# Where a sparse path's small steps stand on GpSimd, VectorE and SyncE in a two-layer encoder

## The chip, the cores and the metric

The kernel runs on one core of a Trainium2 chip. The metric is the device time of one execution in microseconds (us), the median of several runs; lower is better. The engines are TensorE (PE, with PEld for its weight loads), VectorE (DVE), ScalarE (ACT), GpSimd (POOL) and SyncE (SP, which here only issues DMAs).

## The reference

An encoder of two layers over 272 tokens (16 meta tokens and 256 of the input) of 1024 channels. Layer 0 mixes tokens with a gated recurrence, layer 1 with a convolution. Behind each mixer stands the same channel mixer, which picks 16 experts for each of 8 heads and each token, out of 16,384 experts; the change lies in it alone:

```python
def peer_block(xc, w_query, sub_keys, expert_u, expert_v):
    q = (xc @ w_query).reshape(c, PEER_HEADS, 2, PEER_HALF)
    scores = jnp.einsum('chpk,pnk->chpn', q, sub_keys.astype(q.dtype))
    s1, i1 = lax.top_k(scores[:, :, 0], PEER_TOPK)
    s2, i2 = lax.top_k(scores[:, :, 1], PEER_TOPK)
    cand = (s1[..., :, None] + s2[..., None, :]).reshape(c, PEER_HEADS, PEER_TOPK * PEER_TOPK)
    s, flat = lax.top_k(cand, PEER_TOPK)
    ...
    expert = idx1 * PEER_N_KEYS + idx2
    g = jax.nn.softmax(s.astype(jnp.float32), axis=-1).astype(xc.dtype)
    u = expert_u[expert]
    act = jax.nn.gelu(jnp.einsum('chkd,cd->chk', u, xc))
    v = expert_v[expert]
    return jnp.einsum('chk,chkd->cd', g * act, v)
```

The output is all tokens but the 16 meta tokens, in float32.

## The kernel before

**Dense and sparse.** Most tokens are computed densely: TensorE multiplies all 128 tiles of 128 experts of U with the tokens (240 of them), gates the result with one-hot matrices of the picks, and multiplies all 128 tiles of V. Some groups of 16 tokens take a sparse way instead, for the whole or for V alone: rows of U and V are fetched by expert number with indirect DMAs, which GpSimd issues. In layer 0 these groups are tokens 256 to 271 ("early"), 240 to 255 ("late") and 224 to 239 ("drawn"); in layer 1 they are 240 to 255 ("early"), 224 to 239 and 208 to 223 ("drawn"). Each group is a dictionary, `few` in the code. Those that lie below token 256 (all but the first) are called `near`.

**U1 and U2.** The 128 tiles of U are done by two calls of `linears`: tiles 0 to 63 (U1, with `u_store` as what is done to each result) and 64 to 127 (U2, with `u_out`). For each tile `load_split` loads a block of 128x1024 float32 (`raw`, four buffers, issued on SP's queue), ScalarE rounds it (`hi`, three buffers), and the rest `lo = raw - hi` (two buffers) is made by GpSimd for tiles 0 to 40 of U1 and by VectorE from tile 41 (`LO_FROM`) on. TensorE then does 16 matmuls on `hi` (L180, two sorts) and 8 on `lo`, in this order, for each tile. So a late `lo` stops TensorE between the `hi` and the `lo` matmuls of that tile.

**Beside U1**, VectorE picks the experts. `topk_steps` is a generator that yields after each step: 2H steps of maxima over scores, H steps over sums (`cand`), then one-hot steps that turn the found places into key numbers (casts `s`, `pu`, `pf`; comparisons `oh` on L929, products on L935, sums `idx` on L938). It runs whole for tokens 128 to 271 (`picked[0]`), then for tokens 256 to 271 by themselves with H = 1 (`few_topk`, layer 0 only), and for tokens 0 to 127 in the generator `slow`, whose last seven steps are taken one in a tile from tile 41 on. From the key numbers `few_ids` makes the row numbers of the gathers (`ids`).

**Small transfers.** The near groups have their key numbers spread over 128 partitions by way of DRAM: `few_spread` writes `pos` there and `few_fetch` reads it back, both on GpSimd's queue, at tiles 21 (`SPREAD`) and 24 of U1; `few_ids` follows. The softmax weights `z` go the same way near tile 60.

**Gathers.** For the early group, GpSimd fetches 16 rows of U (`few_rows`, L1028) and VectorE multiplies each with its token (`few_mult`, L1035): the first ten from tile 48 of U1 on (`few_dot`), the other six in U2 (`u_out`, L705 to L710), one in four tiles. In U2 `few_dump` also copies finished activations of the drawn groups to DRAM (L723, L724; one buffer `own`).

**The order** on each engine is set by a scheduler when the program is built: an instruction may be placed earlier than it is written, unless `tc.issue_after(x)` puts it behind instruction `x`. On the chip each engine takes its instructions strictly in that order, and waits on semaphores for its inputs.

Of the kernel before, what the change touches and what calls it, by code (L numbers as in the profile page):

```python
# [7 lines left out]
F32 = mybir.dt.float32  # L8
F32R = mybir.dt.float32r
F16 = mybir.dt.float16  # L10
U32 = mybir.dt.uint32
# [6 lines left out]
P = 128  # L18
# [44 lines left out]
class Trunk:  # L63
# [481 lines left out]
    def peer(self, layer, n, xs):  # L545
        tc, nc, a = self.tc, self.nc, self.a
# [9 lines left out]
        with tc.tile_pool(name=f"few{layer}", bufs=1) as kp:  # L556
# [5 lines left out]
            with tc.tile_pool(name=f"top{layer}", bufs=1) as sp:  # L562
# [31 lines left out]
                def u_store(j, ps):  # L594
                    if j == LO_FROM:
                        for few in early:
                            self.few_load(sp, few, "kept", 1)
                    if j >= LO_FROM and len(picked[-1]) == 2:
                        with tc.issue_after(self.dve_lo.ins):
                            try:  # L600
                                next(slow)
                            except StopIteration as end:
                                picked[-1] += end.value
                    k, step = divmod(3 * (j - DOTS_FROM), 4)
                    if early and 0 <= k < DOTS + AHEAD and step < 3:
                        with tc.issue_after(self.dve_lo.ins), tc.issue_after(self.lo_ins.ins):
                            self.few_dot(sp, early[0], k, DOTS, AHEAD)
                    last = nc.scalar.activation(act_a[:, j, :], ps, AF.Gelu_apprx_tanh)
                    i = j - (JA - 6 - 2 * len(picked))
                    t, odd = divmod(i, 2)  # L610
                    if 0 <= t < len(picked) and not odd:
                        c0, m, idx, fv = picked[t]
                        with tc.issue_after(last.ins), tc.issue_after(self.dve_lo.ins):
                            picked[t] = c0, m, idx, self.softmax(sp, fv, P)
                    if j == SPREAD:
                        with tc.issue_after(self.lo_ins.ins):
                            self.few_spread(near, "pos", picked[0][2])
                    if j == JA - 6 - len(picked):
                        with tc.issue_after(last.ins):
                            self.few_spread(near, "z", picked[0][3][:, None])  # L620
                    if j == SPREAD + 3:
                        with tc.issue_after(self.lo_ins.ins):
                            self.few_fetch(near, "pos")
                        for few in near:
                            self.few_ids(few, few["pos"])
                    if j == JA - 2:
                        with tc.issue_after(last.ins):
                            self.few_fetch(near, "z")
                    if t == len(picked) and not odd:
                        with tc.issue_after(last.ins):  # L630
                            for few in early:
                                if few not in near:
                                    self.few_soft(sp, few)
                    if 0 < t <= len(picked) and not odd:
                        with tc.issue_after(last.ins), tc.issue_after(self.mm.ins):
                            self.topk_out(*picked[t - 1], iT, ghT, glT)
                self.linears([U[j] for j in range(JA)], xs, nu, lambda j: FULL if j >= LO_FROM else (("p", 1024),), u_store)

            with tc.tile_pool(name=f"act1{layer}", bufs=1) as ap1:
# [55 lines left out]
                def u_out(i, ps):  # L695
# [7 lines left out]
                        nc.vector.tensor_tensor(w[:, :cd], w[:, :cd], tmp[:, :cd], op=OP.mult)  # L703
                    k, step = divmod(i - 2 + 4 * DOTS, 4)
                    if step == 0 and DOTS <= k < TOPK:  # L705
                        with tc.issue_after(self.dve_lo.ins):
                            early[0]["rows"][k] = self.few_rows(rp, early[0], a["u_rows"], 0, k, 1)
                    if step == 2 and DOTS <= k < TOPK:
                        with tc.issue_after(self.dve_lo.ins):
# [8 lines left out]
                    at[0] = upto  # L718

                def few_dump(few, j, j1):  # L720
                    own = rp.tile([P, 32, FEW], F32, tag="own", name="own", bufs=1)[:, :j1 - j]
                    act, o = (act_a, 0) if j < JA else (act_b, JA)
                    nc.gpsimd.tensor_copy(own, act[:, j - o:j1 - o, few["t0"]:few["t0"] + FEW])  # L723
                    nc.gpsimd.dma_start(few["table"][:, j:j1], own)  # L724
# [160 lines left out]
    def topk_steps(self, sp, sc, m, H, parts=1):  # L885
        nc = self.nc
        K = TOPK
        sv = sp.tile([P, H, 2, K], F32, tag="sv", name="sv", bufs=1)
        si = sp.tile([P, H, 2, K], U32, tag="si", name="si", bufs=1)
# [10 lines left out]
        cand = sp.tile([P, H, K, K], F32, tag="cand", name="cand", bufs=1)  # L900
# [3 lines left out]
        fi = sp.tile([P, H, K], U32, tag="fi", name="fi", bufs=1)  # L904
# [10 lines left out]
        s16 = sp.tile([P, 2, H, K], F16, tag="s16", name="s16", bufs=1)  # L915
        nc.vector.tensor_copy(s16[:m], si[:m].rearrange("p h a k -> p a h k"))
        pu = sp.tile([P, 2, H * K], U32, tag="pu", name="pu", bufs=1)
        fp = fi[:m].rearrange("p h k -> p (h k)")
        nc.vector.tensor_scalar(pu[:m, 0], fp, 4, None, op0=OP.logical_shift_right)
        nc.vector.tensor_scalar(pu[:m, 1], fp, 15, None, op0=OP.bitwise_and)  # L920
        pf = sp.tile([P, 2 * H * K, 2], F16, tag="pf", name="pf", bufs=1)
        nc.vector.tensor_copy(pf[:m], pu[:m].rearrange("p a n -> p (a n)")[:, :, None].to_broadcast([m, 2 * H * K, 2]))
        yield
        oh = sp.tile([P, 2 * H, K, K], F16, tag="cand", name="oh", bufs=1)
# [61 lines left out]
    def few_topk(self, sp, few, q):  # L986
# [18 lines left out]
    def few_spread(self, fews, key, src):  # L1005
        for few in fews:
            self.nc.gpsimd.dma_start(few[key, "far"].rearrange("h t a k -> t a h k"), src[few["t0"] - P:few["t0"] - P + FEW])

    def few_fetch(self, fews, key):
        for few in fews:  # L1010
            self.nc.gpsimd.dma_start(few[key], few[key, "far"].rearrange("h t a k -> (h t) a k"))

    def few_ids(self, few, pos):
        for i in range(2):
# [343 lines left out]
```

## Time and profile before

| | |
|---|---|
| device time, three runs | 1815.02, 1820.03, 1820.5 us; median 1820.03 |
| device time of the profiled execution | 1816.75 us |
| its span, first to last instruction | 1815.0 us, granted TensorE clock 0.987 |
| TensorE busy | 1744.5 us, 96% of the span |
| VectorE, ScalarE, GpSimd busy | 1506.4, 903.2, 545.1 us (83%, 50%, 30%) |

Rows of the profile have the start in us from the span's start, the duration in us, engine, line, operation, output and inputs, and how many instructions are merged; in square brackets stands how long the engine was idle ahead of it and what ended that. Rows of the list of waits have the total, the number of times and the longest. Line numbers are those of the kernel before.

### The profile page before, as it was taken

Reading aid. Unit: us, or ns where it says so; the run is one execution under the profiler, and the core shown is the slowest. Engines: PE = TensorE matmul, PEld = TensorE weight load, DVE = VectorE, ACT = ScalarE, POOL = GpSimd, SP = SyncE. Lnnn points to the kernel's source line nnn. Section 1 sums busy time; section 2 is a strip of 40 time slices with the busy share of each in tenths; the row PEclk is TensorE's granted clock in tenths of the full one; section 3 lists DMA queues with packets and bytes.
Section 4 is the critical chain, followed back from the end, with each engine's and each line's share of the span. In section 5 each row is a group of like instructions: output and inputs, shape, how many; then the busy total and the mean of one; then the engine's idle time right before and its main releaser. Section 6 shows DMA issues by size and latency. Waiting matters only on the chain.

```text
span 1815.0 us, 35001 instructions
## 1 busy us (share of the span) xinstructions
PE 1744.5 (96%) x13468; PEld 1686.4 (93%) x13468; DVE 1506.4 (83%) x2753; ACT 903.2 (50%) x1493; POOL 545.1 (30%) x374
## 2 busy tenths in 40 slices
PE   8999997999999999999998999599999999999997
PEld 7899997999999999999887899599999999999996
DVE  7786999899997888887799869918899978878776
ACT  6554443554445545875532645245554454545552
POOL 1102993210002545431000018681200015643310
PEclk9999998999999999999999999899999999999998
DMA  5445665866557989888441365368765569888884
GB/s 198 163 156 158 198 201 177 284 226 197 172 167 273 337 311 343 316 321 281 174 151 47 111 187 192 119 203 284 237 214 177 169 198 340 310 310 303 319 270 151
DMA packets 115720, 405.91 MB, mean 224 GB/s; under 512 B 14496, under 2 KB 15968, under 8 KB 115424
## 3 DMA queue, kind: packets, MB, share of 16 engines
q1 hardware_dynamic: 91632, 324.74, 53.6%
q0 software_dynamic: 23920, 78.93, 11.9%
q8 instruction: 106, 1.74, 0.4%
q14 instruction: 62, 0.51, 0.1%
HBM read 395.56 MB, written 8.05 MB: 222 GB/s over the span
## 4 chain that ended last, share of the span: by engine, by line
PE 78%; DVE 16%; issue 2%; ACT 1%; POOL 1%; DMA 1%; POOLq 0%; SPq 0%; DVEq 0%; ACTq 0%
PE u L180 36%; PE acc L742 21%; PE acc L746 13%; PE u L216 3%; DVE cy L1238 2%; DVE odd L1238 2%; DVE oh L935 1%; PE g L683 1%; PE g L684 1%; DVE lo L152 1%; POOL lo L152 1%; PE acc L781 1%; DVE x L363 1%; DVE si L898 1%; DVE r L896 0%
## 5 line engine op out<-in xcount | busy, mean ns | idle before, releaser
L145 ACT ACTIVATE hi<-raw 128x1024 fp32r<-128x1024 f32 x556 | 588.0, 1059 | 632.7 <-PE u L180 217.4
L152 DVE TENSOR_TENSOR lo<-raw,hi 128x1024 fp32r<-128x1024 f32 x474 | 577.9, 1224 | 175.0 <-PE u L180 77.2
L180 PE MATMUL u<-xs,hi 128*128 128x240 f32 (+2 forms) x4544 | 571.5, 278 | 0.6 <-DVE xs L379 0.6
L180 PEld LDWEIGHTS u<-xs,hi 128*128 128x128 f32 x4544 | 540.0, 190 | 1.5 <-DVE xs L379 1.2
L742 PE MATMUL acc<-w,hi 128*128 128x448 f32 (+1 forms) x1984 | 431.4, 359 | 2.4 <-DVE w L264 1.9
L742 PEld LDWEIGHTS acc<-w,hi 128*128 128x128 f32 x1984 | 354.4, 189 | 14.4 <-DVE w L264 2.3
L180 PE MATMUL u<-xs,lo 128*128 128x240 f32 (+2 forms) x2272 | 310.5, 278 | 34.5 <-POOL lo L152 21.7
L180 PEld LDWEIGHTS u<-xs,lo 128*128 128x128 f32 x2272 | 282.6, 190 | 36.8 <-POOL lo L152 22.5
L746 PEld LDWEIGHTS acc<-w,lo 128*128 128x128 f32 x2048 | 267.2, 191 | 8.7 <-DVE lo L152 4.9
L746 PE MATMUL acc<-w,lo 128*128 128x224 f32 (+1 forms) x2048 | 269.9, 273 | 3.0 <-DVE lo L152 2.8
L152 POOL TENSOR_TENSOR lo<-raw,hi 128x1024 fp32r<-128x1024 f32 x82 | 208.3, 2558 | 105.1 <-ACT hi L145 79.2
L1028 POOL DMA_INDIRECT rows<-peer_v,ids x96 | 151.1, 1574 | 222.0 <-DVE few_out L1069 138.7
L1028 POOL DMA_INDIRECT rows<-u_rows,ids x48 | 64.3, 1340 | 243.1 <-DVE rows L1035 201.1
L216 PE MATMUL u<-x,raw 128*128 128x272 f32 x480 | 114.5, 399 | 5.2 <-DMA x<-h 5.2
L216 PEld LDWEIGHTS u<-x,raw 128*128 128x128 f32 x480 | 92.9, 194 | 24.5 <-DMA raw<-w_in 5.1
L1069 DVE SCALAR_TENSOR_TENSOR few_out<-rows,act,few_out 128x1024 f32<-128x1024 f32 x90 | 115.2, 1280 | 0.0
L723 POOL COPY own<-act_b 128x512 f32<-128x512 f32 (+2 forms) x9 | 9.2, 1026 | 261.8 <-ACT act_b L699 250.1
L690 ACT ACTIVATE act_b<-g 128x488 f32<-128x488 f32 (+39 forms) x54 | 20.9, 388 | 108.1 <-DVE act_b L653 98.9
L1045 POOL DMA_INDIRECT act<-own,turn x48 | 59.5, 1239 | 25.3 <-DVE turn L1044 13.7
L666 DVE TENSOR_TENSOR AB<-iota,iT 128x2048 f16<-128x2048 f16 x54 | 65.8, 1221 | 0.1
L371 POOL TENSOR_SCALAR xs<-x,par 128x272 fp32r<-128x272 f32 (+1 forms) x4 | 3.5, 878 | 185.3 <-DVE x L363 185.3
L1035 DVE SCALAR_TENSOR_TENSOR rows<-rows,wide 128x1024 f32<-128x1024 f32 x48 | 58.6, 1221 | 0.0
(285 smaller groups left out, 1848.7 us busy)
## 6 DMA issues: line engine op xcount, KB each, us to landing
raw<-peer_u SPq DMA_DIRECT2D x256, 512.0 KB, 3.9
raw<-peer_v SPq DMA_DIRECT2D x248, 512.0 KB, 5.5
raw<-w_query SPq DMA_DIRECT2D x28, 512.0 KB, 3.6
raw<-pw SPq DMA_DIRECT2D x22, 512.0 KB, 3.5
raw<-w_in SPq DMA_DIRECT2D x16, 512.0 KB, 3.8
raw<-w_out SPq DMA_DIRECT2D x8, 512.0 KB, 4.2
raw<-peer_v SPq DMA_DIRECT2D x16, 256.0 KB, 4.3
wide<-wide SPq DMA_DIRECT2D x5, 512.0 KB, 5.0
```

Of the source, the lines that this page charges most:

```text
L145: self.act_hi = nc.scalar.activation(hi, raw, AF.Copy).ins
L152: i = e.tensor_tensor(lo[:, s], raw[:, s], hi[:, s].bitcast(F32), op=OP.subtract)
L180: self.mm = nc.tensor.matmul(ps[:, :n], l[:, k, :], xs(k, r)[:, :n], start=start, stop=stop)
L216: self.mm = self.nc.tensor.matmul(ps[:, :n], raw[:, k, :], x[:, k, :n], start=k == 0, stop=k == NB - 1)
L666: nc.vector.tensor_tensor(AB.rearrange("p x c (a b) -> p (x c) a b", b=2), keys, iT[:, c0 // HC].rearrange("p x c b -> p (x c) b")[:, :, N ...
L742: self.mm = nc.tensor.matmul(acc[b][:, :2 * n].rearrange("p (a t) -> p a t", a=2), hi, w[:, :, :n], start=j == 0, stop=j == NK - JG - 1, s ...
L746: self.mm = nc.tensor.matmul(main[b][:, :n], hi if p_ else lo, w[:, i, :n], start=False, stop=j == NK - 1 and not p_, skip_group_check=True)
L1028: self.nc.gpsimd.indirect_dma_start(out=t, out_offset=None, in_=table, in_offset=bass.IndirectOffsetOnAxis(ap=few["ids"][:, i, k:k + 1], a ...
L1035: self.nc.vector.scalar_tensor_tensor(t, t, 1.0, few["x"], op0=OP.mult, op1=OP.mult, accum_out=few["act"][:, k:k + 1])
L1045: self.nc.gpsimd.indirect_dma_start(out=few["act"][:, k:k + 1], out_offset=None, in_=few["table"].rearrange("p j (t o) -> (p j t) o", o=1) ...
L1069: nc.vector.scalar_tensor_tensor(few["out"], t, w, few["out"], op0=OP.mult, op1=OP.add)
L1238: nc.vector.scalar_tensor_tensor(z, h, w, z, op0=OP.mult, op1=OP.add)
```

## The change

1. In `u_out` the gather of rows 10 to 15 is ordered behind `lo_ins`, the last `lo` that GpSimd made (tile 40 of U1), instead of `dve_lo`, VectorE's latest.
2. The `pos` spreads and fetches are issued on SP's queue, behind the load of tile 21 and of tile 25, instead of on GpSimd's.
3. `few_topk` takes only three steps at once; the five that are left (the one-hot steps) follow from tile 41 on, two in a tile (`few_picked`), and `slow` waits until they are done. `few_ids` of the near groups stands behind VectorE's `lo` of tiles 42, 43 (and 44 in layer 1).
4. The scratch tiles of `topk_steps` have one set of buffers for H = 8 and one for H = 1, and the last piece of `few_dump` has buffers of its own.

```diff
+                    behind = [few for few in early if few.get("left")]
+                    if j >= LO_FROM and behind:
+                        with tc.issue_after(self.dve_lo.ins):
+                            for _ in range(min(2, behind[0]["left"])):
+                                self.few_picked(behind[0])
-                    if j >= LO_FROM and len(picked[-1]) == 2:
+                    elif j >= LO_FROM and len(picked[-1]) == 2:
...
                     if j == SPREAD:
-                        with tc.issue_after(self.lo_ins.ins):
-                            self.few_spread(near, "pos", picked[0][2])
+                        with tc.issue_after(self.last_load):
+                            self.few_spread(nc.sync, near, "pos", picked[0][2])
...
-                    if j == SPREAD + 3:
-                        with tc.issue_after(self.lo_ins.ins):
-                            self.few_fetch(near, "pos")
-                        for few in near:
-                            self.few_ids(few, few["pos"])
+                    if j == SPREAD + 4:
+                        with tc.issue_after(self.last_load):
+                            self.few_fetch(nc.sync, near, "pos")
+                    if LO_FROM < j <= LO_FROM + len(near):
+                        with tc.issue_after(self.dve_lo.ins):
+                            self.few_ids(near[j - LO_FROM - 1], near[j - LO_FROM - 1]["pos"])
...
                     if step == 0 and DOTS <= k < TOPK:
-                        with tc.issue_after(self.dve_lo.ins):
+                        with tc.issue_after(self.lo_ins.ins):
                             early[0]["rows"][k] = self.few_rows(rp, early[0], a["u_rows"], 0, k, 1)
...
-                    own = rp.tile([P, 32, FEW], F32, tag="own", name="own", bufs=1)[:, :j1 - j]
+                    tail = j1 - j <= 8
+                    own = rp.tile([P, 8 if tail else 32, FEW], F32, tag="tail" if tail else "own", name="own", bufs=1 + tail)[:, :j1 - j]
...
-        sv = sp.tile([P, H, 2, K], F32, tag="sv", name="sv", bufs=1)
+        sv = sp.tile([P, H, 2, K], F32, tag=f"sv{H}", name="sv", bufs=1)
...
-        steps = self.topk_steps(sp, sc, P, 1)
-        while True:
-            try:
-                next(steps)
-            except StopIteration as done:
-                idx, few["fv"] = done.value
-                break
-        self.few_ids(few, idx[:, :, 0])
+        few["steps"] = self.topk_steps(sp, sc, P, 1)
+        for _ in range(3):
+            next(few["steps"])
+        few["left"] = 5
+
+    def few_picked(self, few):
+        few["left"] -= 1
+        try:
+            next(few["steps"])
+        except StopIteration as done:
+            idx, few["fv"] = done.value
+            self.few_ids(few, idx[:, :, 0])
```

**GpSimd in layer 1, U1, before.** `x22` is the `lo` of tiles 0 to 21; the ninth row is row 10 of the early group, written in U2.

```order
L152 TENSOR_TENSOR lo<-raw,hi 128x1024 x22
L1007 DMA pos_240_12501<-idx 32x8x16
L1007 DMA pos_224_12508<-idx 32x8x16
L1007 DMA pos_208_12515<-idx 32x8x16
L152 TENSOR_TENSOR lo<-raw,hi 128x1024 x3
L1011 DMA pos_12500<-pos_240_12501 128x32
L1011 DMA pos_12507<-pos_224_12508 128x32
L1011 DMA pos_12514<-pos_208_12515 128x32
L1028 DMA rows<-u_rows,ids_12497 128x1024
L152 TENSOR_TENSOR lo<-raw,hi 128x1024 x9
L723 COPY own<-act_a 128x512
L724 DMA own_224_15076<-own 128x512
```

Behind these stand seven more `lo`. GpSimd in layer 1, U1, now:

```order
L378 TENSOR_SCALAR x_10623<-x_10623,par 128x256
L152 TENSOR_TENSOR lo<-raw,hi 128x1024 x41
L1039 DMA rows<-u_rows,ids_12497 128x1024 x8
L1018 DMA z_240_12502<-z 16x8x16
L1018 DMA z_224_12509<-z 16x8x16
```

All 41 `lo` stand in one row, and the first gather behind them. The dump of `own` that stood among them has moved to the start of U2, where four dumps instead of three now stand ahead of the gather of row 11. In layer 0 the two spreads and two fetches are gone from among the `lo` in the same way.

**VectorE in layer 0, before:** the one-hot steps of tokens 256 to 271 (sizes 128x16 to 128x512) between the maxima of `slow`, while GpSimd makes `lo`.

```order
L919 TENSOR_SCALAR pu<-fi 128x16
L920 TENSOR_SCALAR pu<-fi 128x16
L898 MAX_INDEX si<-sv,r 128x8
L922 CAST pf<-pu 128x64
L894 MAX sv<-sc 128x8
L929 TENSOR_TENSOR oh<-iota_98,pf 128x512
L895 MAX_INDEX si<-sv,sc 128x8
L935 TENSOR_TENSOR oh<-oh,s_1901 128x512
L896 MATCH_REPLACE r<-sv,sc 128x128
L938 TENSOR_REDUCE idx<-oh 128x32
L897 MAX sv<-r 128x8
L1020 TENSOR_SCALAR ids_1619<-idx 128x16 x2
```

VectorE in layer 0, now, from its first `lo` (tile 41) on:

```order
L152 TENSOR_TENSOR lo<-raw,hi 128x1024
L923 CAST s_3425<-si 128x32
L926 TENSOR_SCALAR pu<-fi 128x16
L927 TENSOR_SCALAR pu<-fi 128x16
L929 CAST pf<-pu 128x64
L936 TENSOR_TENSOR oh<-iota_98,pf 128x512
L152 TENSOR_TENSOR lo<-raw,hi 128x1024
L942 TENSOR_TENSOR oh<-oh,s_3425 128x512
L1031 TENSOR_SCALAR ids_1622<-pos_1625 128x16 x2
L945 TENSOR_REDUCE idx<-oh 128x32
L1032 TENSOR_TENSOR ids_1622<-ids_1622,pos_1625 128x16 x2
L152 TENSOR_TENSOR lo<-raw,hi 128x1024
```

The steps stand between the `lo` of tiles 41, 42 and 43. The maxima and the sums of the small group (H = 1) now stand a little ahead of the sum `idx` of tokens 128 to 271.

**SP in layer 0, now** (six loads of tiles 0 to 5 come ahead of these rows; before, they were one row of 62 loads):

```order
L135 DMA raw<-peer_u 128x1024 x16
L1018 DMA pos_240_1626<-idx 32x8x16
L1018 DMA pos_224_1633<-idx 32x8x16
L135 DMA raw<-peer_u 128x1024 x4
L1022 DMA pos_1625<-pos_240_1626 128x32
L1022 DMA pos_1632<-pos_224_1633 128x32
L135 DMA raw<-peer_u 128x1024 x42
```

The spreads, which wait for `idx`, stand between the loads of tiles 21 and 22, the fetches between those of 25 and 26; layer 1 has three of each at the same places. In layer 1 the second load of the early group's tokens (`wide`, L645) has moved on SP from the load of tile 0 to behind that of tile 67, where layer 0 has it in both versions. The orders on TensorE and ScalarE are the same in both.

More of the change, by code (lines that the diff above doesn't have):

```diff
@@ L615, in u_store @@
                     if j == SPREAD:
-                        with tc.issue_after(self.lo_ins.ins):
-                            self.few_spread(near, "pos", picked[0][2])
+                        with tc.issue_after(self.last_load):
+                            self.few_spread(nc.sync, near, "pos", picked[0][2])
                     if j == JA - 6 - len(picked):
                         with tc.issue_after(last.ins):
-                            self.few_spread(near, "z", picked[0][3][:, None])
-                    if j == SPREAD + 3:
-                        with tc.issue_after(self.lo_ins.ins):
-                            self.few_fetch(near, "pos")
-                        for few in near:
-                            self.few_ids(few, few["pos"])
+                            self.few_spread(nc.gpsimd, near, "z", picked[0][3][:, None])
+                    if j == SPREAD + 4:
[4 more added lines that the diff above has]
+                            self.few_ids(near[j - LO_FROM - 1], near[j - LO_FROM - 1]["pos"])
                     if j == JA - 2:
                         with tc.issue_after(last.ins):
-                            self.few_fetch(near, "z")
+                            self.few_fetch(nc.gpsimd, near, "z")
                     if t == len(picked) and not odd:
@@ L887, in topk_steps @@
         K = TOPK
-        sv = sp.tile([P, H, 2, K], F32, tag="sv", name="sv", bufs=1)
-        si = sp.tile([P, H, 2, K], U32, tag="si", name="si", bufs=1)
+        sv = sp.tile([P, H, 2, K], F32, tag=f"sv{H}", name="sv", bufs=1)
+        si = sp.tile([P, H, 2, K], U32, tag=f"si{H}", name="si", bufs=1)
         for b in range(2 * H):
@@ L899, in topk_steps @@
             yield
-        cand = sp.tile([P, H, K, K], F32, tag="cand", name="cand", bufs=1)
+        cand = sp.tile([P, H, K, K], F32, tag=f"cand{H}", name="cand", bufs=1)
         nc.vector.tensor_tensor(cand[:m], sv[:m, :, 0, :, None].to_broadcast([m, H, K, K]),
@@ L903, in topk_steps @@
         fv = sp.tile([P, H, K], F32, tag="fv", name="fv", bufs=4)
-        fi = sp.tile([P, H, K], U32, tag="fi", name="fi", bufs=1)
+        fi = sp.tile([P, H, K], U32, tag=f"fi{H}", name="fi", bufs=1)
         for h in range(H):
@@ L914, in topk_steps @@
             yield
-        s16 = sp.tile([P, 2, H, K], F16, tag="s16", name="s16", bufs=1)
+        s16 = sp.tile([P, 2, H, K], F16, tag=f"s16{H}", name="s16", bufs=1)
         nc.vector.tensor_copy(s16[:m], si[:m].rearrange("p h a k -> p a h k"))
-        pu = sp.tile([P, 2, H * K], U32, tag="pu", name="pu", bufs=1)
+        pu = sp.tile([P, 2, H * K], U32, tag=f"pu{H}", name="pu", bufs=1)
         fp = fi[:m].rearrange("p h k -> p (h k)")
@@ L920, in topk_steps @@
         nc.vector.tensor_scalar(pu[:m, 1], fp, 15, None, op0=OP.bitwise_and)
-        pf = sp.tile([P, 2 * H * K, 2], F16, tag="pf", name="pf", bufs=1)
+        pf = sp.tile([P, 2 * H * K, 2], F16, tag=f"pf{H}", name="pf", bufs=1)
         nc.vector.tensor_copy(pf[:m], pu[:m].rearrange("p a n -> p (a n)")[:, :, None].to_broadcast([m, 2 * H * K, 2]))
         yield
-        oh = sp.tile([P, 2 * H, K, K], F16, tag="cand", name="oh", bufs=1)
+        oh = sp.tile([P, 2 * H, K, K], F16, tag=f"cand{H}", name="oh", bufs=1)
         idx = sp.tile([P, 2, H, K], F32, tag=f"idx{H}", name="idx", bufs=2)
@@ L995, in few_topk, with few_spread, few_fetch @@
         nc.scalar.activation(sc, ps[:, :2], AF.Copy)
-        steps = self.topk_steps(sp, sc, P, 1)
-        while True:
-            try:
-                next(steps)
-            except StopIteration as done:
-                idx, few["fv"] = done.value
-                break
-        self.few_ids(few, idx[:, :, 0])
-    def few_spread(self, fews, key, src):
+        few["steps"] = self.topk_steps(sp, sc, P, 1)
[9 more added lines that the diff above has]
+            self.few_ids(few, idx[:, :, 0])
+    def few_spread(self, queue, fews, key, src):
         for few in fews:
-            self.nc.gpsimd.dma_start(few[key, "far"].rearrange("h t a k -> t a h k"), src[few["t0"] - P:few["t0"] - P + FEW])
-    def few_fetch(self, fews, key):
+            queue.dma_start(few[key, "far"].rearrange("h t a k -> t a h k"), src[few["t0"] - P:few["t0"] - P + FEW])
+    def few_fetch(self, queue, fews, key):
         for few in fews:
-            self.nc.gpsimd.dma_start(few[key], few[key, "far"].rearrange("h t a k -> (h t) a k"))
+            queue.dma_start(few[key], few[key, "far"].rearrange("h t a k -> (h t) a k"))
     def few_ids(self, few, pos):
```

## The prediction

> **What bounds the kernel now.** I read the page's busy times and the chain of work that ended last, and then TensorE's list of waits.
>
> ```profile
> PE 1744.5 (96%) x13468; PEld 1686.4 (93%) x13468; DVE 1506.4 (83%) x2753; ACT 903.2 (50%) x1493; POOL 545.1 (30%) x374
> PE 78%; DVE 16%; issue 2%; ACT 1%; POOL 1%; DMA 1%; POOLq 0%; SPq 0%; DVEq 0%; ACTq 0%
> PE u L180 <- POOL lo L152: 21.7, 4, 18.7
> PE u L180 <- DVE lo L152: 12.8, 4, 10.3
> PE mu L342 <- DVE total L875: 6.9, 1, 6.9
> ```
>
> TensorE is the bound: busy for 96% of the span, and 78% of the chain. So only what lets TensorE stand still can pay, and the list has two such places in the matmuls of U (L180): 21.7 us behind GpSimd's `lo`, of which 18.7 in one wait, and 12.8 behind VectorE's, of which 10.3 in one. No other edit can bring more than a few us, since the next wait in the list, 6.9, is in code that the change leaves alone. I then read the timeline around those two waits.
>
> **Layer 1, tile 25: the gather among the `lo`.**
>
> ```profile
> 1157.98 1.96 PE L180 MATMUL u<-xs,hi 128*128 128x240 f32 x16
> 1178.59 2.06 PE L180 MATMUL u<-xs,lo 128*128 128x240 f32 x8 [18.65 <-POOL lo L152]
> 1185.01 1.96 PE L180 MATMUL u<-xs,hi 128*128 128x240 f32 x16
> 1156.18 1.68 POOL L1011 DMA_DIRECT2D pos<-pos  x3
> 1174.84 0.23 DVE L1017 TENSOR_SCALAR ids<-pos,slot 128x16 uint32<-128x16 f32 x1
> 1175.12 1.04 POOL L1028 DMA_INDIRECT rows<-u_rows,ids  x1 [17.26 <-DVE ids L1017]
> ```
>
> GpSimd issued its three fetches until 1157.86, then stood 17.26 us at the gather of row 10, whose row numbers VectorE made only at 1174.84, behind its maxima. The `lo` of tile 25 stood behind that gather, and TensorE behind this `lo`. From the `hi` matmuls at 1157.98 to those of two tiles later, at 1185.01, go 27.03 us. A tile takes 2.69 undisturbed (282.30 to 284.99, next fence), so the stall costs 27.03 - 5.38 = 21.65: the wait of 18.65, and 3.0 of slower matmuls behind it.
>
> With the change the 41 `lo` stand in one piece and the gather behind them. Nothing of VectorE's then stands in GpSimd's queue during U1, and the 21.65 go whole. What is late next is tile 41, where VectorE takes over. VectorE's ids at 1174.84 are its last work of this kind, and tile 41's `lo` is needed some 16 tiles behind tile 25, that is at about 1158 + 16 x 2.69 = 1201. The cover is 26 us.
>
> **Layer 0, tile 41: VectorE is late.**
>
> ```profile
> 282.30 1.95 PE L180 MATMUL u<-xs,hi 128*128 128x240 f32 x16
> 284.99 1.95 PE L180 MATMUL u<-xs,hi 128*128 128x240 f32 x16
> 297.20 2.06 PE L180 MATMUL u<-xs,lo 128*128 128x240 f32 x8 [10.27 <-DVE lo L152]
> 302.36 1.97 PE L180 MATMUL u<-xs,hi 128*128 128x240 f32 x16
> 224.72 1.86 DVE L919 TENSOR_SCALAR pu<-fi 128x16 uint32<-128x16 uint32 x1
> 226.85 2.13 DVE L922 CAST pf<-pu 128x64 f16<-128x64 uint32 x1
> 229.10 2.46 DVE L929 TENSOR_TENSOR oh<-iota,pf 128x512 f16<-128x512 f16 x1
> 231.75 21.27 DVE L935 TENSOR_TENSOR oh<-oh,s 128x512 f16<-128x512 f16 x1
> 253.21 0.67 DVE L938 TENSOR_REDUCE idx<-oh 128x32 f32<-128x512 f16 x1
> 254.00 1.41 DVE L1020 TENSOR_SCALAR ids<-idx 128x16 uint32<-128x16 f32 x2
> 255.60 2.44 DVE L1021 TENSOR_TENSOR ids<-ids,idx 128x16 uint32<-128x16 uint32 x2
> 295.93 1.23 DVE L152 TENSOR_TENSOR lo<-raw,hi 128x1024 fp32r<-128x1024 f32 x1
> 252.91 2.39 POOL L152 TENSOR_TENSOR lo<-raw,hi 128x1024 fp32r<-128x1024 f32 x1 [0.18 <-ACT hi L145]
> 303.76 1.22 DVE L935 TENSOR_TENSOR oh<-oh,s 128x2048 f16<-128x2048 f16 x1
> ```
>
> From 284.99 to 302.36 two tiles take 17.37 instead of 5.38: 11.99 us are lost, because VectorE made its first `lo` (tile 41) at 295.93. That buffer is free when TensorE has done tile 39, at 282.30. TensorE needs the `lo` behind the `hi` matmuls of 284.99, at 284.99 + 1.79 = 286.8. So VectorE must be free by 286.8 - 1.2 = 285.6, some 10 us earlier than it was.
>
> What the change takes from ahead of tile 41 are the seven quoted steps: 1.86 + 2.13 + 2.46 + 21.27 + 0.67 + 1.41 + 2.44 = 32.2, nearly all of it L935, which ended within 0.3 us of the first gap (0.18, ahead of 252.91) in GpSimd's run of `lo`. The same operation on four times the elements took 1.22 at 303.76, when GpSimd made none. So I read it as shut out by GpSimd while that goes from one `lo` to the next. VectorE is then free at 295 - 32 = 263, with 22 us of cover.
>
> The Trainium skill ("SBUF — State Buffer", section "SBUF: two separate sides") has the port that these two engines share as a lock that is held for one whole instruction. One `lo` is 2.39 by the row, so by that rule L935 should have waited some 2.4 and not 21.27, and nine in a row speak against the lock going to the one that waits. If no more than 2.4 of it were the port's doing, and the rest vanished for another cause, the sum would be the same; if the rest went along with the step, it is the third rival below.
>
> The moved steps have to go beside VectorE's own `lo` from tile 41 on, two steps a tile, with no GpSimd `lo` any more. They are small: a quarter of the 1.22 for L935, the others no longer than quoted, so 11.3 us over three tiles (1.86 + 2.13 + 2.46 + 0.3 + 0.67 + 1.41 + 2.44). A tile gives 2.69 - 1.23 = 1.46 free, and the lead is 286.8 less 283.5, when the first `lo` may be done: 3.3. Taken at the quoted durations they would cost 11.3 - 3 x 1.46 - 3.3 = 3.6. But those durations stem from contention too (quoted 0.23 for an ids operation at 1174.84, against 0.7 at 254.00), and at a third of them nothing is lost. Bounds 0 and 3.6; I take 0.3, nearer the uncontended row. Steps of the slow tokens come three tiles later each, in free time of the same size: 0.
>
> Sum of gains: 21.65 + 11.99 = 33.64.
>
> **SP's new waits.**
>
> ```profile
> 217.01 4.42 DVE L938 TENSOR_REDUCE idx<-oh 128x256 f32<-128x4096 f16 x1
> 221.59 0.33 SPq L135 DMA_DIRECT2D raw<-peer_u  x1
> 224.22 0.33 SPq L135 DMA_DIRECT2D raw<-peer_u  x1
> 227.81 1.07 ACT L145 ACTIVATE hi<-raw 128x1024 fp32r<-128x1024 f32 x1 [1.32 <-DMA raw<-peer_u]
> 231.22 1.47 POOL L1007 DMA_DIRECT2D pos<-idx  x2
> DMA to landing us min/median/max: 3.1/3.4/3.8
> 219.25 1.16 PE L180 MATMUL u<-xs,lo 128*128 128x240 f32 x8 [1.41 <-POOL lo L152]
> 1137.64 1.16 PE L180 MATMUL u<-xs,lo 128*128 128x240 f32 x8 [1.41 <-POOL lo L152]
> ```
>
> The spreads now stand on SP between the loads of tiles 21 (221.59) and 22 (224.22), and wait for `idx`, which ended at 221.43. The small group's first steps stand ahead of `idx` now, so I add 2 to 4.5 us: 223.4 to 226. Behind the waiting spread stands load 22; two spreads at about 0.7 each (1.47 for two on GpSimd) put it at 224.8 to 227.4. How late may it be? The `hi` of tile 22 ran to 228.88, while GpSimd was ready for it at 231.22, where it now has no spread to issue: 2.3 us. TensorE needs that `lo` at 282.30 - 18 x 2.69 + 1.79 = 235.7, and 231.22 + 2.4 = 233.6 leaves another 2.1. So load 22 may be issued as late as 224.22 + 4.4 = 228.6. Nothing is lost, by 1.2 us at the worst. The fetches stand behind load 25, two periods and more after load 23; the spreads have landed 3.1 to 3.8 after their issue, by 231 at the latest, and load 25 goes out at about 231.3. A wait there is under the same 4.4. In layer 1 no small group stands ahead of `idx`: 0. I take 0 for all four places, with 0 to 2 as bounds.
>
> The two waits of 1.41 (219.25, 1137.64) are beside the one-hot work of tokens 128 to 271, which stays, and I leave them in.
>
> **U2 in layer 1.**
>
> ```profile
> 1290.47 0.62 POOL L723 COPY own<-act_a 128x512 f32<-128x512 f32 x1 [2.91 <-DMA own<-own]
> 1295.88 0.61 POOL L723 COPY own<-act_a 128x512 f32<-128x512 f32 x1 [3.93 <-DMA own<-own]
> 1297.86 1.22 POOL L1028 DMA_INDIRECT rows<-u_rows,ids  x1 [0.52 <-DVE rows L1035]
> 1309.01 1.22 DVE L1035 SCALAR_TENSOR_TENSOR rows<-rows,wide 128x1024 f32<-128x1024 f32 x1
> rows<-u_rows,ids POOLq DMA_INDIRECT x48, 6.2
> 1287.80 1.16 PE L180 MATMUL u<-xs,lo 128*128 128x240 f32 x8 [0.63 <-DVE lo L152]
> 363.34 1.17 PE L180 MATMUL u<-xs,lo 128*128 128x240 f32 x8 [1.50 <-DVE lo L152]
> ```
>
> A dump is paced by the single buffer `own`: 1295.88 - 1290.47 = 5.41. With a fourth dump ahead, the gather of row 11 goes out at up to 1297.86 + 5.4 = 1303.3, and lands 6.2 later, at 1309.5, where its multiplication began at 1309.01: 0.5 late, on VectorE, which has free time in each tile; the upper bound is 1.5. The moved load `wide` makes layer 1's start of U2 like layer 0's: 1.50 instead of 0.63 at the most. I take 0.5 for both together. The dumps' own new buffers save waits of GpSimd alone, with the next gather bound by TensorE anyway: 0.
>
> **The sum.** -33.64 + 0.3 + 0.5 = -32.8. The profiled execution took 1816.75, 3.3 under the median of the three runs (1820.03). Against its own time: 1784.0; with those 3.3: 1787.2. As three runs spread over 5.5 I place the median a little toward the own time: 1786.
>
> **Rivals.**
>
> *Only layer 1 gains.* VectorE stays late in layer 0 because the maxima of the slow tokens, which run on under GpSimd's `lo`, stretch to fill what was freed. For it: L935 shows that VectorE can be held up for 21 us there. Against it: 22 us of cover. 1816.75 - 21.65 + 0.8 = 1795.9, and 1799 as median. Chance 0.10.
>
> *The wait moves and nothing is gained.* The gather's place is taken by another wait in GpSimd's queue or SP's, of about the same size in each layer. For it: VectorE's ids and `idx` are as late as before. Against it: the new order shows no row on GpSimd among the 41 `lo`. 1820. Chance 0.04.
>
> *The 21 us go along with the one-hot step.* L935 was slow for a cause of its own, and is slow behind tile 41 again. VectorE would be late by 21.27 less the lead of 3.3 and a tile's free 1.46, that is 16.5, plus 1.72 of slow matmuls (11.99 - 10.27): 18.2 where 12.0 were lost. 1816.75 - 21.65 + 6.2 + 0.8 = 1802.1, 1805 as median. Against it: 1.22 for four times the elements. Chance 0.04. The rule of the Trainium skill above speaks for this one.
>
> *Slower: SP becomes the bound.* Its spreads and fetches hold up the loads behind them, at four places. A place costs what it waits over the 4.4 us worked out above, plus 2 to 3 of slow matmuls; to take back 32.8 each must wait about 32.8 / 4 + 4.4 - 2.5 = 10 us. At 20 us a place the loss would be 4 x (20 - 4.4 + 2.5) = 72, less 32.8: 1816.75 + 39.6 = 1856. The longest landing quoted is 3.8, and `idx` ends within 4.5 us of its old time, which speaks against. It decides if `idx` ends past 224.2 + 10 = 234 and the other three waits are as long. Chance 0.04.
>
> **How the numbers follow.** Both stalls gone: 0.78, between 1779 (the two waits of 1.41 go as well, no cost comes, and the lowest of the runs shown, 1815.02, is the level: 1815 - 33.6 - 2.8) and 1794 (the upper bounds in place of the values taken: 3.6 + 2 + 1.5 + 0.9, over 1786). With the first rival's 1799 and its own spread the range is 1779 to 1801; outside lie the other three rivals, 0.12. About 0.3%, 5.5 us, is what a measurement tells from no change here. Faster: 0.78 + 0.10 + 0.04 = 0.92; same 0.04; slower 0.04.
>
> **What would show it.** In the profile after, TensorE's waits for GpSimd's `lo` should fall from 21.7 to about 3, and for VectorE's from 12.8 to about 3. The gathers' wait for `ids` (17.26) should be gone or lie behind tile 40. L935 on 128x512 should take about 0.3 to 0.5, between the `lo` of tiles 42 and 43. SP's loads of tile 22 should be issued by 228.6 in layer 0, with no wait of TensorE for tiles 22 to 26. The prediction is wrong if a wait on `hi` or `raw` shows there, if VectorE's `lo` of tile 42 to 44 comes late by more than 3 us, or if VectorE isn't at tile 41's `lo` by 285.6.

## The result, and the profile after

| | before | changed |
|---|---|---|
| device time, median of four runs | 1818.38 us (1815.02 to 1820.5) | 1795.19 us (1792.22 to 1795.91) |
| ratio | | 0.987, 95% interval 0.985 to 0.989 |
| profiled execution, its span | 1816.75, 1815.0 us | 1794.91, 1793.1 us |

The change gains 23 us, inside the range; the time given as likeliest was 1786, 9 us lower. The page of the changed kernel has the same busy times for TensorE, and a larger share of TensorE in the chain of work that ended last:

```profile
PE 1743.2 (97%) x13468; PEld 1685.1 (94%) x13468; DVE 1469.1 (82%) x2753; ACT 903.6 (50%) x1493; POOL 552.3 (31%) x364
PE 82%; DVE 9%; DMA 3%; ACT 2%; issue 2%; POOL 1%; POOLq 0%; DVEq 0%; SPq 0%; ACTq 0%
```

TensorE's list of waits shows both stalls gone, and a new one of 3.9 us:

```profile
PE mu L342 <- DVE total L882: 7.0, 1, 7.0
PE u L180 <- DVE lo L152: 5.9, 3, 3.9
PE u L216 <- DMA x<-h: 5.2, 1, 5.2
PE u L180 <- POOL lo L152: 3.0, 3, 1.4
```

The waits of U's matmuls fell from 34.5 us to 8.9. The timeline at the two places of the prediction, TensorE and VectorE at tile 41 of layer 0, then TensorE at tile 25 of layer 1:

```profile
285.63 1.96 PE L180 MATMUL u<-xs,hi 128*128 128x240 f32 x16
291.01 1.17 PE L180 MATMUL u<-xs,hi 128*128 128x240 f32 x9
283.31 1.23 DVE L152 TENSOR_TENSOR lo<-raw,hi 128x1024 fp32r<-128x1024 f32 x1 [22.50 <-PE u L180]
287.14 0.41 DVE L942 TENSOR_TENSOR oh<-oh,s 128x512 f16<-128x512 f16 x1
...
1147.38 1.95 PE L180 MATMUL u<-xs,hi 128*128 128x240 f32 x16
1152.95 1.28 PE L180 MATMUL u<-xs,hi 128*128 128x240 f32 x10
```

Two tiles take 5.38 us instead of 17.37 in layer 0, and 5.57 instead of 27.03 in layer 1. VectorE stood idle for 22.50 us ahead of its first `lo` (22 of cover were forecast), and the product of 128x512 (L942, L935 before) took 0.41 us. SP's spreads went out at 222.57 and load 22 at 224.54, and TensorE waits for no `raw` or `hi` behind them.

What was lost again stands at the start of U2 in layer 1. GpSimd's queue and VectorE there, and TensorE:

```profile
1231.31 0.94 POOL L1039 DMA_INDIRECT rows<-u_rows,ids  x1 [1.89 <-DVE rows L1046]
1236.35 1.70 POOL L1018 DMA_DIRECT2D z<-z  x3 [4.11 <-DVE d L957]
1241.00 1.68 POOL L1022 DMA_DIRECT2D z<-z  x3 [2.96 <-DMA z<-z]
1242.98 1.93 POOL L1039 DMA_INDIRECT rows<-u_rows,ids  x1 [0.30 <-DVE lo L152]
1245.22 1.14 POOL L1039 DMA_INDIRECT rows<-u_rows,ids  x1 [0.31 <-issue]
...
1233.18 0.29 DVE L965 TENSOR_TENSOR z<-z,sm 128x128 f32<-128x128 f32 x1
1249.55 1.22 DVE L1046 SCALAR_TENSOR_TENSOR rows<-rows,wide 128x1024 f32<-128x1024 f32 x1 [2.90 <-DMA rows<-u_rows,ids]
1252.44 1.23 DVE L1046 SCALAR_TENSOR_TENSOR rows<-rows,wide 128x1024 f32<-128x1024 f32 x1 [0.52 <-DMA rows<-u_rows,ids]
...
1253.16 1.95 PE L180 MATMUL u<-xs,hi 128*128 128x240 f32 x16
1259.00 1.20 PE L180 MATMUL u<-xs,lo 128*128 128x240 f32 x8 [3.89 <-DVE lo L152]
1260.00 3.57 PE L180 MATMUL u<-xs,hi 128*128 128x240 f32 x16
1264.31 0.95 PE L180 MATMUL u<-xs,hi 128*128 128x240 f32 x7
```

The chain reads from top to bottom. VectorE's `z` was done at 1233.47, and the trace records no other wait of the spread that was still open, yet GpSimd issued it at 1236.35, 2.88 us later. In the kernel before it went out 0.30 behind `z` (1265.83 behind 1265.53), with the same steps of VectorE beside it. The releaser that the row names, L957, ended in between; the spread does not read what it makes. The fetch stands behind the spread's landing, the gathers of rows 8 and 9 behind the fetch. VectorE waits 2.90 and 0.52 us for their rows, is late with the `lo` of tile 64, and TensorE waits 3.89 us and runs slowly for a tile (3.57). From 1253.16 to 1264.31 go 11.15 us, where the kernel before took 6.27 (1285.22 to 1291.49). The same places in the kernel before:

```profile
1265.24 0.29 DVE L958 TENSOR_TENSOR z<-z,sm 128x128 f32<-128x128 f32 x1
1265.83 1.69 POOL L1007 DMA_DIRECT2D z<-z  x3 [1.53 <-DVE z L958]
...
1285.22 1.95 PE L180 MATMUL u<-xs,hi 128*128 128x240 f32 x16
1291.49 1.95 PE L180 MATMUL u<-xs,hi 128*128 128x240 f32 x16
```

The second loss is at the very end. A table of busy time by stretch, the changed kernel and then the kernel before (columns: stretch, its length, busy time of PE, PEld, DVE, ACT and POOL with instructions, TensorE's clock, DMA share, GB/s):

```profile
1780.00:1786.50 6.50, 0.00 (x0) 0.00 (x0) 2.03 (x2) 0.41 (x1) 3.15 (x2) 0.50 0.43 161
1786.50:1793.10 6.60, 0.00 (x0) 0.00 (x0) 0.00 (x0) 0.00 (x0) 0.00 (x0) 0.50 0.00 0
```

```profile
1807.00:1813.70 6.70, 0.00 (x0) 0.00 (x0) 2.43 (x3) 0.81 (x2) 3.27 (x2) 0.50 0.42 157
1813.70:1815.00 1.30, 0.00 (x0) 0.00 (x0) 0.00 (x0) 0.00 (x0) 0.00 (x0) 0.50 0.00 0
```

The last output byte has landed at 1786.2 (1813.6 before). Behind it the kernel before ends within 1.4 us; the changed one has 6.6 us in which no engine and no DMA works. The views leave instructions that only wait out; the trace's records of them name it. GpSimd's last drain, an instruction behind which all engines meet at the end of the program, ends 9.17 us behind GpSimd's last operation; in the kernel before it ended 1.73 behind it. From TensorE's last matmul to the end go 17.76 us instead of 12.22.

### The profile page after: what moved, and what is told of

The parts are those of the page before. It is cut to its first block, busy times and chain, and to the rows that moved or that the text cites. A ratio compares the mean times of both kernels' runs of the same rounds, so it can differ in the third digit from the quotient of the medians.

```text
span 1793.1 us, 35004 instructions
## 1 busy us (share of the span) xinstructions
PE 1743.2 (97%) x13468; PEld 1685.1 (94%) x13468; DVE 1469.1 (82%) x2753; ACT 903.6 (50%) x1493; POOL 552.3 (31%) x364
## 4 chain that ended last, share of the span: by engine, by line
PE 82%; DVE 9%; DMA 3%; ACT 2%; issue 2%; POOL 1%; POOLq 0%; DVEq 0%; SPq 0%; ACTq 0%
PE u L180 41%; PE acc L749 20%; PE acc L753 12%; PE u L216 3%; DVE cy L1249 2%; DVE odd L1249 2%; DMA raw<-peer_v 1%; PE g L689 1%; PE g L690 1%; DVE lo L152 1%; POOL lo L152 1%; PE sps L578 1%; PE acc L788 1%; ACT hi L145 1%; DVE x L363 1%
## 5 line engine op out<-in xcount | busy, mean ns | idle before, releaser
L1039 POOL DMA_INDIRECT rows<-u_rows,ids x48 | 69.4, 1445 | 216.0 <-DVE rows L1046 169.0
```

The source lines that it names most:

```text
L1039: self.nc.gpsimd.indirect_dma_start(out=t, out_offset=None, in_=table, in_offset=bass.IndirectOffsetOnAxis(ap=few["ids"][:, i, k:k + 1], a ...
```

## The experiments

All ratios are to the kernel before, run on the same chip. The kernels were run on several chips, so kernels of different chips are better compared by their ratios.

**One edit alone: the gather.** Kernel before, with

```diff
-                        with tc.issue_after(self.dve_lo.ins):
+                        with tc.issue_after(self.lo_ins.ins):
                             early[0]["rows"][k] = self.few_rows(rp, early[0], a["u_rows"], 0, k, 1)
```

> The kernel before with one edit alone: the U2 gathers ordered behind GpSimd's last lo. Theory: TensorE's 18.65 us wait at tile 25 of layer 1 goes (21.5 us with the slow matmuls behind it), and the 10.27 us wait at tile 41 of layer 0 stays: about 1797 us against 1818. Theory on what was lost at the start of U2 in layer 1 (TensorE waited 3.89 us with the whole change, 0.63 before): it comes from the softmax weights' transfers on GpSimd standing ahead of the gathers of rows 8 and 9, and shows here too if those transfers start more than 2 us behind VectorE's z; then 1801 to 1802. Rival: it comes from the edits that this kernel lacks, and the wait here is 0.6. GpSimd's last drain took 4.4 us before and 11.9 with the whole change: if the number of DMAs on its queue decides that, it is 4.4 here; if it varies from run to run, either.

Measured 1796.3 us, ratio 0.988 (0.987 to 0.990). The wait of layer 1 is gone, that of layer 0 stays, at 7.59 us:

```profile
230.83 18.85 DVE L935 TENSOR_TENSOR oh<-oh,s 128x512 f16<-128x512 f16 x1
231.78 7.10 POOL L152 TENSOR_TENSOR lo<-raw,hi 128x1024 fp32r<-128x1024 f32 x3
238.81 1.14 POOL L1011 DMA_DIRECT2D pos<-pos  x2
239.96 14.46 POOL L152 TENSOR_TENSOR lo<-raw,hi 128x1024 fp32r<-128x1024 f32 x6
254.72 2.40 POOL L152 TENSOR_TENSOR lo<-raw,hi 128x1024 fp32r<-128x1024 f32 x1 [0.29 <-PE u L180]
293.65 2.06 PE L180 MATMUL u<-xs,lo 128*128 128x240 f32 x8 [7.59 <-DVE lo L152]
```

At the start of U2 TensorE waited 0.63 us, `z` went out 0.30 behind VectorE, and the last drain was 1.73 behind the last operation. So the order of the gathers costs nothing there, and both losses come with the other edits. The row of L935 also corrects the prediction: it ended at 249.68, inside GpSimd's run of six `lo` (239.96 to 254.42) and not at a gap. The `lo` that began at 249.37 took 2.58 us instead of 2.4. Its inputs had been ready only 0.15 us before the `lo` ahead of it ended: GpSimd had nearly caught up with TensorE, and its next `lo` was no longer ready early. The product had waited over seven `lo`, and the two issues of `pos` fetches among them had not let it in either.

**The split of the one-hot steps undone.** Changed kernel, with

```diff
-        for _ in range(3):
-            next(few["steps"])
-        few["left"] = 5
+        few["left"] = 8
+        for _ in range(8):
+            self.few_picked(few)
```

> The changed kernel with the small group's one-hot steps at once again, as before the change, all other edits kept. Theory: the 21 us product step was shut out while GpSimd went from lo to lo without a gap; with the pos transfers off GpSimd's queue it has gaps of 0.29 us from 232.0 us on, so the product of 128x512 ends at the first gap, in under 8 us, VectorE is at tile 41 in time, and the time is within 3 us of the changed kernel's 1795. Rival: moving those steps behind tile 41 is what freed VectorE; then the product again takes some 21 us, TensorE waits about 10 us at tile 41 of layer 0, and the time is about 1807.

Measured 1796.0 us, ratio 0.989 (0.987 to 0.990): the same as the changed kernel, and no wait at tile 41. VectorE's product and GpSimd:

```profile
229.52 2.35 DVE L942 TENSOR_TENSOR oh<-oh,s 128x512 f16<-128x512 f16 x1
231.79 2.39 POOL L152 TENSOR_TENSOR lo<-raw,hi 128x1024 fp32r<-128x1024 f32 x1 [0.21 <-POOL lo L152]
```

2.35 us instead of 21.27, still among GpSimd's `lo`. Without the pos transfers in its queue (1.47 and 1.14 us) GpSimd catches up at 231.6 instead of 252.7. So in layer 0 the stall goes without the split, and the gap that lets the product in stands where the pos transfers were. Pos was not moved by itself, though: the own buffers of point 4 of the change are in this kernel too, and they put the product 2.2 us earlier (229.52 instead of 231.75). What those buffers do alone was not tried.

**Pos on GpSimd again.** Changed kernel, with the spread at tile 21 and the fetch at tile 24 as before:

```diff
-                        with tc.issue_after(self.last_load):
-                            self.few_spread(nc.sync, near, "pos", picked[0][2])
+                        with tc.issue_after(self.lo_ins.ins):
+                            self.few_spread(nc.gpsimd, near, "pos", picked[0][2])
...
-                    if j == SPREAD + 4:
-                        with tc.issue_after(self.last_load):
-                            self.few_fetch(nc.sync, near, "pos")
+                    if j == SPREAD + 3:
+                        with tc.issue_after(self.lo_ins.ins):
+                            self.few_fetch(nc.gpsimd, near, "pos")
```

> The changed kernel with the pos spreads and fetches on GpSimd's queue again, at the places of the kernel before; the row numbers are still made behind tile 41. Theory: both large waits stay away, since GpSimd waits for nothing of VectorE's between its lo but the idx of tile 21; 0.3 us more at tile 22 of layer 1 at most. If the number of DMAs on GpSimd's queue sets its last drain, that is 4.4 us again instead of 11.9 and the time is about 5 us lower, 1790; else 1795. Rival: without the move to SP GpSimd comes late, and TensorE waits for its lo 3 us or more in each layer: 1801.

Measured 1786.4 us, ratio 0.983 (0.981 to 0.985), 9 us below the changed kernel and 10 below the kernel with the split undone, which ran on the same chip. VectorE's product still took 0.42 us:

```profile
287.20 0.42 DVE L942 TENSOR_TENSOR oh<-oh,s 128x512 f16<-128x512 f16 x1
```

So the split, again with the buffers of point 4, removes layer 0's stall as well, with pos where it was. The drain is 1.73 and `z` goes out 0.30 behind VectorE. TensorE's wait at tile 64 is 2.35 all the same. My expectation of 1790 had the drain and not the prompt `z`.

**The fetch of `z` later.** Changed kernel; the fetch leaves tile 62 of U1 for U2, where it stands behind the gather of row 11 (`self.gather`, the last gather that `few_rows` issued):

```diff
-                    if j == JA - 2:
-                        with tc.issue_after(last.ins):
-                            self.few_fetch(nc.gpsimd, near, "z")
...
+                    if i == 8:
+                        with tc.issue_after(self.gather.ins):
+                            self.few_fetch(nc.gpsimd, near, "z")
```

> The changed kernel with the fetch of the softmax weights moved on GpSimd from tile 62 of U1 to behind the gather of row 11 in U2. Theory: the gathers of rows 8 and 9 in layer 1 go out 2 us or more earlier, VectorE's waits for them (2.90 and 0.52 us) go, its lo of tile 64 is in time, and TensorE's wait there falls from 3.89 to under 0.8 us, with the slow matmuls behind it: 4 to 5 us less, about 1790.5. Rival: the wait comes from the four copies of own or the moved load of wide at the start of U2, which both stay: no change, 1795.

Measured 1791.2 us, ratio 0.986 (0.984 to 0.988). The spread is as late as in the changed kernel, but the gathers no longer stand behind the fetch:

```profile
1235.50 1.70 POOL L1018 DMA_DIRECT2D z<-z  x3 [4.11 <-DVE d L957]
1237.71 1.01 POOL L1039 DMA_INDIRECT rows<-u_rows,ids  x1 [0.50 <-DVE z L960]
1255.23 1.17 PE L180 MATMUL u<-xs,lo 128*128 128x240 f32 x8 [0.85 <-DVE lo L152]
```

TensorE's wait is 0.85 instead of 3.89. That settles where most of the loss at U2's start came from: the gathers behind the `z` transfers, not the copies of `own` nor `wide`, which both stay. It is not the whole account of this wait. Where `z` is prompt and the fetch in its old place, the wait runs from 0.63 to 2.35 in the kernels here, and with the late fetch from 0.85 to 1.61; what sets the rest is not shown.

**What makes `z` late and the drain long.** The next kernels vary how many DMAs stand on GpSimd's queue. Pos on GpSimd together with the late fetch (227 DMAs):

> The changed kernel with both edits: pos on GpSimd's queue again, and the fetch of the softmax weights behind the gather of row 11. Theory: the two gains add. GpSimd's last drain is 4.4 us again (5.5 us less than with the whole change), and TensorE's wait at tile 64 of layer 1, 2.35 us with pos on GpSimd, falls under 0.9: 1784, 1.5 to 3 us under the 1786.4 with pos on GpSimd alone. Rival: the later fetch brings nothing there, since the z transfers were not delayed in that kernel: 1786.

1787.6 us, 0.984 (0.982 to 0.987): no gain over pos on GpSimd alone. The rival held for the time, though TensorE's wait at tile 64 fell from 2.35 to 1.36. The late fetch, issued three times (`for _ in range(3):`; 227):

> The kernel with the late fetch of the softmax weights (pos on SP), but with each fetch issued three times: ten DMAs more on GpSimd's queue, 227 in all, as before the change; they write the same values again. Theory on the last drain: the number of DMAs on GpSimd's queue decides it, so it is 4.4 us and not 11.9, and in spite of the added work the time is 4 to 6 us lower than the 1791.2 of that kernel: 1786. Rival: what counts is that the pos transfers stand on GpSimd's queue in U1; the drain stays 11.9 us, and the time is 1791 to 1793.

1786.3 us, 0.984 (0.981 to 0.986): the kernel with the late fetch and ten useless transfers more is 4 to 5 us faster. The two ran on different chips and their intervals just overlap; the traces decide, since from TensorE's last matmul to the end go 12.58 us instead of 17.77. Pos on SP in one layer only (`nc.sync if layer == 0 else nc.gpsimd`, and the reverse):

> The changed kernel with pos on SP in layer 0 only; in layer 1 it is on GpSimd's queue, 223 DMAs there in all. Theory that plain transfers in U1 of layer 1 keep GpSimd's later ones prompt: z in layer 1 goes out within 0.4 us of VectorE's last step on it (2.6 us late with the whole change), and the last drain is 4.4 us: 1787 to 1789. Rival, the count: whether 223 lies on the side of 217 or of 227 decides the drain, and the z transfers may be late with a short drain or the reverse.

1786.0 us, 0.983 (0.981 to 0.985): `z` is prompt, and the drain is 1.3.

> The changed kernel with pos on SP in layer 1 only; in layer 0 it is on GpSimd's queue, 221 DMAs there in all. Theory that plain transfers in U1 of layer 1 matter: z in layer 1 goes out some 2.6 us late and the last drain is 11.9 us, as with the whole change: about 1794. Rival, the count: 221 decides, so that the drain may be 4.4 us though z is late.

1783.3 us, 0.982 (0.979 to 0.985): the theory that plain transfers must stand in U1 of layer 1 falls, since here there are none, and `z` is prompt and the drain short. To try the number by itself, nothing was moved and transfers were only added (in U2 of layer 0, the fetch of `z` again, twice in one kernel and once in the other, behind the changed kernel run once more):

```diff
+                    if i == 8 and layer == 0:
+                        with tc.issue_after(self.gather.ins):
+                            for _ in range(2):
+                                self.few_fetch(nc.gpsimd, near, "z")
```

> The changed kernel itself once more, for its times beside those of the next three. If the late z transfers in layer 1 (2.88 us behind VectorE's last step on z, 0.30 elsewhere) and the long last drain (9.2 us behind GpSimd's last operation, 1.0 to 1.7 elsewhere) belong to this program, both are here again and the time is 1795; if they vary from run to run, one of them is gone.

1793.9 us, 0.988 (0.986 to 0.990): both losses are there again, `z` 2.88 late and the drain 9.16.

> The changed kernel with nothing taken away: the fetch of the softmax weights in layer 0 is issued twice more, in U2, behind the gather of row 11 (four small DMAs on GpSimd's queue, 221 in all; they write the same values again). Theory that the number of DMAs on GpSimd's queue decides: z in layer 1 goes out 0.30 us behind VectorE instead of 2.88, TensorE's wait at tile 64 falls from 3.89 to under 1 us, the last drain falls from 9.2 to 1.0 to 1.7 us behind the last operation: 1786, some 9 us faster for four useless transfers. Rival, that the pos transfers must stand on GpSimd's queue: nothing changes, 1795.

1785.5 us, 0.984 (0.982 to 0.986), 8 us below the changed kernel on the same chip. `z` in layer 1, TensorE at tile 64, and the stretch behind the last output byte:

```profile
1232.01 1.70 POOL L1022 DMA_DIRECT2D z<-z  x3 [1.52 <-DVE z L969]
1254.61 1.17 PE L180 MATMUL u<-xs,lo 128*128 128x240 f32 x8 [1.04 <-DVE lo L152]
1782.00:1783.50 1.50, 0.00 (x0) 0.00 (x0) 0.00 (x0) 0.00 (x0) 0.00 (x0) 0.50 0.00 0
```

The wait falls from 3.89 (4.17 in the repeat) to 1.04 and the empty stretch from 6.6 to under 2 us.

> The same with one more fetch, two DMAs, 219 in all. If the number decides, this tells on which side of 219 the change lies, and whether the late z and the long drain go together: 1786 if both are gone, 1795 if both stay, about 1790 with one of them.

1792.7 us, 0.987 (0.985 to 0.989): the drain is still long, `z` is prompt, and the wait at tile 64 is 2.02. The two don't go together. Here another DMA, a gather just ahead, started late: it is the 114th on the queue, as `z` is in the changed kernel. Its row stands first here, then the 114th with four more transfers, then the 114th with pos on SP in layer 1 only:

```profile
1230.36 1.89 POOL L1043 DMA_INDIRECT rows<-u_rows,ids  x1 [3.23 <-DVE d L961]
1219.69 0.94 POOL L1043 DMA_INDIRECT rows<-u_rows,ids  x1 [3.23 <-DVE lo L152]
1217.93 0.94 POOL L1039 DMA_INDIRECT rows<-u_rows,ids  x1 [1.75 <-DVE rows L1046]
```

Counted from the end of the multiplication that frees their buffer, and not as the idle time in the brackets, the first two went out after 1.75 us, where the gathers next to them need 0.27; in the second kernel, as in the one with the fetch three times, the late gather stands so far ahead that `z` is prompt. The third went out after 0.27, though its kernel has 221 DMAs like the second. So the number ahead of it does not make the 114th late by itself.

| kernel | DMAs on GpSimd's queue | `z` behind VectorE, layer 1 | drain behind GpSimd's last operation |
|---|---|---|---|
| changed (three profiles with 217: changed, again, split undone) | 217 | 2.88 us | 9.2 us |
| late fetch | 217 | 2.88 | 9.2 |
| two more transfers | 219 | 0.30 | 9.3 |
| four more; pos on SP in layer 1 only; the same with late fetch | 221 | 0.30 | 0.8, 1.0, 1.0 |
| pos on SP in layer 0 only | 223 | 0.30 | 1.3 |
| before; gather alone; pos on GpSimd, without and with late fetch; fetch three times | 227 | 0.30 | 1.7; in the last 1.3 |

**Late fetch on the fastest.** Pos on SP in layer 1 only, with the late fetch:

> The fastest so far (pos on SP in layer 1 only, 1783.3) with the late fetch of the softmax weights. Theory: in that kernel z goes out promptly and TensorE waits only 0.69 us at tile 65 of layer 1 and 1.50 at tile 64 of layer 0, so the later fetch can bring 1 us at the most: 1782 to 1784. Rival: the gathers of rows 8 and 9 still bind there, and 2 us or more go: 1781.

1787.0 us, 0.984 (0.982 to 0.986). No gain, as the theory had it; the interval takes in the other's 0.982. The lowest version beside the changed one is pos on SP in layer 1 only, 1783.3 us, some 10 us below the changed kernel, with runs from 1779.6 to 1790.9; it cannot be told apart from those at 1785 to 1787.

## Why the prediction was right, and where its size was off

The sum was made against the profiled execution: 1816.75 - 32.8 = 1784.0. It took 1794.91, 10.9 more. By terms, from the two traces:

| term | forecast | measured |
|---|---|---|
| layer 1, tile 25 | -21.65 us | -21.5 (27.03 to 5.57 for two tiles) |
| layer 1, tile 22 (short wait behind the pos spread) | not named | -0.5 |
| layer 0, tile 41 | -11.99 | -12.0 (17.37 to 5.38) |
| moved one-hot steps | +0.3 | 0 |
| SP's four waits | 0 | 0 |
| start of U2 in layer 1 | +0.5 | +4.9 (6.27 to 11.15) |
| behind the last matmul | none | +5.5 (12.22 to 17.76) |
| layer 0, tiles 56 and 58 | none | +1.0 |
| all the rest | none | +0.7 |

*The range.* For both stalls gone the prediction gave 1779 to 1794. The median of 1795.19 lies above that, and inside the whole range of 1779 to 1801 only because the range was drawn wide enough for the first rival, in which layer 0 stays as it was. That rival did not come true. So the mechanism was right, and that the number fell inside was partly luck.

*The stalls.* Both went, and their sizes were right to 0.2 us. The gather's effect is shown by itself (20 us of the median by that edit alone). The 22 us of cover at tile 41 are there as 22.50 in VectorE's row.

*The credit in layer 0.* The prediction gave the 12 us to the seven steps moved behind tile 41. The runs show that either is enough, that move or pos off GpSimd's queue, each with the own buffers of point 4, which were not tried by themselves. Together they bring what each brings. The reading "shut out by GpSimd" held: 2.35, 18.85 and 21.27 us for one operation, depending on when GpSimd catches up. The nine `lo` in a row of the prediction were eight, with the two issues of `pos` fetches among them (239.77 to 240.91), where the product did not get in either; with the gather's edit alone they were seven. The rival that the 21 us go along with the step is out: 0.41 there. The Trainium skill's rule ("SBUF — State Buffer", section "SBUF: two separate sides") has the port held for one whole instruction of the engine that started first. The 2.35 us agrees with a wait for one such instruction, the 18.85 and 21.27 don't.

*SP.* The spread was at 222.57 and load 22 at 224.54, earlier than the 224.8 to 227.4 forecast. `idx` ended at 222.11, only 0.7 us later than before (221.43), where 2 to 4.5 had been added for the small group's first steps.

*U2 in layer 1, the step that failed.* I priced the fourth copy of `own` ahead of row 11 and the moved load, at 0.5 together and at most 2.4. What became late were rows 8 and 9, two gathers earlier, behind `z` transfers that the change does not touch. They cost 4.9 us where 0.5 was put. TensorE's waits for VectorE's `lo` were forecast at about 3; the list has 5.9.

*The end of the program, the term that was missing.* Nothing was put for what lies behind the last matmul, and it grew by 5.5 us. I had counted what the ten DMAs cost where they were taken away and where they were put, and nothing for the queue that had them before.

*Tiles 56 and 58.* TensorE's transposes of `z` wait 0.39 and 0.42 us for VectorE, which now is later there; before, they came without a wait. It is seen, not tried.

The rival in which only layer 1 gains gave 1799 (1795.9 against the profiled execution); the gather's edit alone, where only layer 1 gains, measured 1796.3.

What stays open is why GpSimd starts its 114th DMA late in seven of these kernels and not in the others, and why its drain ends some 8 us later with 217 or 219 DMAs than with 221 to 227. A fixed capacity of that queue that has to be gone round is a guess; how a count far from these behaves was not tried.

## What to carry to other kernels

Read the end of the span in two traces before a sum is closed: what lies behind the last matmul differs by 5.5 us between kernels that do the same work there. When small transfers leave a queue, look at what follows on that queue to the end of the program, and try one or two transfers more or fewer; it costs a line. And undo each part by itself: here either of two edits was enough for the same stall, and leaving one of them out, pos on SP, makes the kernel 9 us faster.

## What the runs showed of the hardware that I had not expected

Four useless transfers of 8 KB on GpSimd's queue made the kernel 8 us faster (1793.9 to 1785.5 us). GpSimd's last drain took 9.2 to 9.3 us behind its last operation with 217 and 219 DMAs on its queue, in five profiles, and 0.8 to 1.7 with 221, 223 and 227, in nine. A VectorE product of 128x512 took 0.41 us with no `lo` of GpSimd beside it, and 2.35, 18.85 or 21.27 us among them, the longer the later GpSimd caught up.
